# A layer's first stage from a channel-major copy of the input: squares summed by products, the scale applied by GpSimd

## The chip, the cores and the metric

The kernel runs on one core of a Trainium2 chip. A core has TensorE (PE) for matrix products, VectorE (DVE), ScalarE (ACT) and GpSimd (POOL) for work on tiles of 128 partitions, and SyncE (SP), whose queue issues nearly all transfers between HBM and the core's SBUF. Products land in PSUM. The engines run on their own, each through its instructions in order, and wait for one another by semaphores. The metric is the device time of one execution in microseconds (us); the median of the runs counts.

## What is computed

One layer of a decoder over 1024 positions of 1024 channels. What the change touches is its beginning:

```python
mod = c_act @ w_ada[l] + b_ada[l]              # c_act = silu(c)
sh1, sc1, g1, sh2, sc2, g2 = split(mod, 6)
h = rms_norm(x, pre_mix_g[l]) * (1.0 + sc1) + sh1
y = token_mixer(h, w_in[l], ...)               # begins with h @ w_in
x = x + g1 * rms_norm(y, post_mix_g[l])
...                                            # gated MLP with its own norm, shift and gain
```

`rms_norm` divides each position by the root of the mean square over its channels. All of it is float32; a product is made of three products of rounded parts (`hi` by `hi`, `hi` by `lo`, `lo` by `hi`).

## The kernel before

A product on TensorE sums over partitions, so `h` is wanted with channels on partitions: `xT`, 8 chunks of 128 channels (index `k`) by 1024 positions. `hT[t]` holds `h` for half `t` of the positions (512) in two parts: `hThi`, rounded by ACT, and the rest `hTlo`, which DVE makes by a subtraction.

The front (in the code between `front = tc.manual_schedule()` and `front.__exit__`) runs in the order in which it is written, on every engine. Behind it a planner sets the order. The front does this:

- SP's queue loads x in 8 blocks of 128 positions (`x_load`), the column constants `cv`, the rows of `w_ada` (512 KB for each of the 48 groups of modulation values, `ada_pair(k)` loads the two for chunk `k`), and the first units of `w_in`.
- For each block `b`, `x_square` (ACT, with a sum along each row) and `rstd_of` (two small POOL operations) make 1/rms; `x_turn` scales the block on DVE and transposes it in 8 pieces on PE; `x_evac` copies the pieces from PSUM to `xT`, on ACT or DVE.
- The shift and the gain of chunk `k` are `mod[:, k]` and `g_mix[:, k]`. For chunk 0 they come from products on PE (`ada_product`, 16 products of one column for each of the two); for the others from `ada_sums`: DVE multiplies the 128x1024 tile of `w_ada` by the conditioning `cb`, spread to all partitions, with a sum along each row (`ada_sum`, L168), and `shift_gain` follows in two small DVE operations.
- `h_part(k, t)` makes `h` of chunk `k`: scale and shift (DVE for chunk 0, ACT for the others), the cast to `hThi` on ACT, the rest on DVE.
- `h_chunk(k)` prepares chunk `k + 1` and sums for chunk `k + 2`, while PE runs the 48 products of chunk `k`: 8 blocks by two units of `w_in` (`kv` and `v`) by the three terms. Each product has a weight load of its own and 256 columns. `first_split` makes the two parts of the first two units, in halves: the first before chunk 0, the second in `h_chunk(0)`.

After the 384 products, `token_group` continues with the products `tg`. POOL has nothing from the last 1/rms until the front's end, but for eight tiny memsets.

Of the kernel before, what the change touches and what calls it, by code (L numbers as in the profile page):

```python
# [10 lines left out]
F32 = mybir.dt.float32  # L11
# [7 lines left out]
P = 128  # L19
# [38 lines left out]
def layer_kernel(  # L58
    ctx: ExitStack,
    tc: tile.TileContext,  # L60
    x: bass.AP,
    w_ada: bass.AP,
    c: bass.AP,
    ccol: bass.AP,
    w_vg: bass.AP,
    w_in: bass.AP,
    w_out: bass.AP,
# [11 lines left out]
    def f(ap):  # L79
        return ap.bitcast(F32)  # L80
# [12 lines left out]
    def rstd_of(dst, ssq, n):  # L93
        G.tensor_scalar(dst, ssq, 1.0 / n, EPS, op0=ALU.mult, op1=ALU.add)  # L94
        G.tensor_tensor(dst, dst, neghalf[:, : dst.shape[1]], op=ALU.pow)
# [32 lines left out]
    def block_tile(b, name):  # L128
        return mixp.tile([P, MIXC], F32, tag=f"mix{b}", name=name)
# [77 lines left out]
    xs = [block_tile(b, f"x{b}")[:, :D] for b in range(NB)]  # L207

    def x_load(b):
        nc.sync.dma_start(xs[b], x[b * P : (b + 1) * P, :])  # L210

    def ada_tile(i, j):
        i = i if i < 10 else (i - 10) ^ 1
        if i < 2:
# [25 lines left out]
    nc.scalar.dma_start(cc8, ccol)  # L240
# [16 lines left out]
    ada_pair(3)

    def x_square(b):
        A.activation(hT[1][1][:, 6:8, :], xs[b].rearrange("p (a b) -> p a b", a=2), AF.Square, accum_out=ssq[:, b : b + 1])  # L260
        rstd_of(rst[:, b : b + 1], ssq[:, b : b + 1], D)

    xps = {}

    def x_turn(b):
        V.tensor_scalar(xs[b], xs[b], rst[:, b : b + 1], None, op0=ALU.mult)
        for h in range(2):
            ps = xps[b, h] = (mm, pB)[h](f"xtp{b}")
            for i in range(4):
                T.transpose(ps[:, i * P : (i + 1) * P], xs[b][:, (4 * h + i) * P : (4 * h + i + 1) * P], ident)  # L270

    def x_evac(b, h, copy):
        copy(xT[:, 4 * h : 4 * h + 4, b * P : (b + 1) * P], xps[b, h].rearrange("p (a b) -> p a b", a=4))

    def shift_gain(k):
        c = slice(k, k + 1)
        V.tensor_tensor(mod[:, c], mod[:, c], cv[:, C_BADA + k : C_BADA + k + 1], op=ALU.add)
        V.scalar_tensor_tensor(g_mix[:, c], mod[:, 8 + k : 9 + k], cv[:, C_PREMIX + k : C_PREMIX + k + 1], gb[:, c], op0=ALU.mult, op1=ALU.add)

    def h_part(k, t):  # L280

        c = slice(k, k + 1)
        hk = xT[:, k, 512 * t : 512 * (t + 1)]
        hi, lo = (part[:, k, :] for part in hT[t])
        return (
            lambda: A.activation(hk, hk, AF.Identity, bias=mod[:, c], scale=g_mix[:, c]),
            lambda: V.tensor_scalar(hk, hk, g_mix[:, c], mod[:, c], op0=ALU.mult, op1=ALU.add),
            lambda: A.copy(hi, hk),
            lambda: V.tensor_tensor(lo, hk, f(hi), op=ALU.subtract),
        )  # L290

    C_, D_ = A.copy, V.tensor_copy
    x_square(0)
# [3 lines left out]
    A.activation(tc8, cc8, AF.Tanh, scale=0.5)  # L297
    V.scalar_tensor_tensor(cc8, tc8, 1.0, cc8, op0=ALU.add, op1=ALU.mult)
    V.tensor_scalar(cc8, cc8, 0.5, None, op0=ALU.mult)
# [6 lines left out]
    x_turn(0)  # L306
    x_square(1)
    x_turn(1)
    x_square(2)
    for h in range(2):  # L310
        A.copy(cb[:, 512 * h : 512 * (h + 1)], cbs[h])
    x_evac(0, 1, D_)
    mps = []

    def ada_product(j):

        if not mps:
            mps.append(pA("mod0"))
        for k in range(KD):
            T.matmul(mps[0][:, j : j + 1], adas[j][:, k * P : (k + 1) * P], cc8[:, k : k + 1], start=k == 0, stop=k == KD - 1)  # L320

    for b in range(2, NB):
        x_turn(b)
        if b + 1 < NB:
            x_square(b + 1)
        x_evac(b - 2, 0, C_)
        x_evac(b - 1, 1, D_ if b < 6 else C_)
        if b == 5:

            V.scalar_tensor_tensor(gb, cv[:, C_BADA + 8 : C_BADA + 16], 1.0, cv[:, C_PREMIX : C_PREMIX + 8], op0=ALU.add, op1=ALU.mult)  # L330
            ada_product(8)
        if b == 6:
            ada_product(0)
    V.tensor_tensor(mod[:, 0:1], mps[0][:, 0:1], cv[:, C_BADA : C_BADA + 1], op=ALU.add)
# [23 lines left out]
    for _ in ada_sums(1):  # L358
        pass

    def h_chunk(k):

        if k and k + 3 < KD:
            ada_pair(k + 3)
        sums = ada_sums(k + 2) if k + 2 < KD else iter(())
        if k + 1 < KD:
            for t in range(2):
                act, _, cast, rest = h_part(k + 1, t)
                act()
                cast()  # L370
                next(sums, None)
                rest()
        next(sums, None)
# [43 lines left out]

    for k in range(KD):
        h_chunk(k)
        for n, b in passes(k):  # L420
                hi, lo = hT[b // 4]
                ts = slice((b % 4) * P, (b % 4 + 1) * P)
                uh, ul = (part[:, (k % 4) * 256 : (k % 4 + 1) * 256] for part in units[2 * (k // 4) + n])
                ps = (pkv, pv)[n][b // 2][:, 256 * (b % 2) : 256 * (b % 2 + 1)]

                mm3(ps, hi[:, k, ts], lo[:, k, ts], uh, ul, k == 0 and b % 2 == 0, k == KD - 1 and b % 2 == 1)
# [885 lines left out]
def _columns(v):  # L1312
    return v.reshape(-1, P).T


def _layout(inputs):
# [30 lines left out]
        ],  # L1347
        axis=1,
    )
    w_ada = np.ascontiguousarray(g["w_ada"][0].T)  # L1350
    for j in (0, 8):

        b = slice(j * P, (j + 1) * P)
        w_ada[b] = g["w_ada"][0][:, b].reshape(KD, P, P).transpose(1, 0, 2).reshape(P, D)
    rows = np.concatenate([g["ml_i_b"][0], g["ml_f_b"][0], g["attn_sinks"][0]])[None, :]
    return {
        "x": g["x"].reshape(S, D),
        "w_ada": w_ada,
        "c": g["c"].reshape(1, D),
        "ccol": _columns(g["c"]),  # L1360
        "w_vg": w_vg,
        "w_in": np.concatenate(parts, axis=0),
        "w_out": g["w_out"][0],
# [23 lines left out]
```

## Time and profile before

| | |
|---|---|
| runs | 1128.68, 1127.90, 1127.55 us; median 1127.9 |
| profiled execution | 1128.73 us; from first to last instruction (span) 1126.7 |
| PE busy | 1110.8 us, 99% of the span |
| DVE / ACT / POOL busy | 75% / 50% / 13% |
| granted clock of TensorE, mean | 0.996 |
| first product of the front (`kv`) | 26.42 us after the span's start |
| first product behind the front (`tg`) | 75.35 us |

A row of the trace in order of time reads: start in us, duration, engine, line of the kernel, operation, what it writes and reads, shapes; in brackets the idle time of that engine before it and what ended it. A row of the chain has start, duration and the engine with tile and line. A window row has, for one stretch, the busy time and number of instructions of PE, PE's weight loads, DVE, ACT and POOL, then the granted clock as a share of full speed, the share of the DMA engines in use, and GB/s.

### The profile page before, as it was taken

To read this page: it belongs to the slowest core of one execution; us is meant where nothing else is said; L and a number is where in the kernel's file an instruction comes from. 1 tells how busy PE (TensorE), PEld (TensorE's weight loads), DVE (VectorE), ACT (ScalarE), POOL (GpSimd) and SP (SyncE) were. 2 spreads that over 40 slices of the span, in tenths; PEclk is the share of its full clock that TensorE was granted. 3 is DMA by queue.
4 is the path that set the end of the run, shared out by engine and by line. 5 is a ranking of instruction groups with operands and counts; after the bars stand their busy time and mean duration, and the time that the engine had idled before them with its cause. 6 is when DMAs were issued, how large, how long until landed. Compare 5 with 4: busy or idle time off the path is not lost.

```text
span 1126.7 us, 16175 instructions
## 1 busy us (share of the span) xinstructions
PE 1110.8 (99%) x5949; PEld 943.7 (84%) x5949; DVE 846.0 (75%) x1510; ACT 563.2 (50%) x1133; POOL 150.3 (13%) x227
## 2 busy tenths in 40 slices
PE   7999999999999999999999999999999999999997
PEld 6999998888899888877788888888888888888886
DVE  4946879857665456798897888879787877777686
ACT  6642534655535345575553545445454555454552
POOL 2012334554334100000000000000000000000021
PEclk8999999999999999999999999999999999999999
DMA  9625526242103222323333233233313359633445
GB/s 355 236 96 178 166 77 188 94 150 75 38 20 108 100 93 94 113 79 127 103 122 111 67 122 107 72 102 122 121 56 113 132 182 359 230 116 103 150 127 210
DMA packets 55166, 146.85 MB, mean 130 GB/s; under 512 B 5464, under 2 KB 5808, under 8 KB 55088
## 3 DMA queue, kind: packets, MB, share of 16 engines
q1 hardware_dynamic: 53056, 140.31, 37.2%
q10 hardware_dynamic: 2032, 5.51, 1.2%
q8 instruction: 47, 0.77, 0.3%
q14 instruction: 31, 0.25, 0.1%
HBM read 117.19 MB, written 28.61 MB: 129 GB/s over the span
## 4 chain that ended last, share of the span: by engine, by line
PE 90%; DVE 5%; ACT 2%; DMA 2%; issue 1%; POOL 0%; DVEq 0%; POOLq 0%; ACTq 0%
PE X L1036 7%; PE X L1035 7%; PE X L1037 7%; PE Y L1036 4%; PE Y L1037 4%; PE Y L1035 4%; PE dx L1217 3%; PE dx L1215 3%; PE dx L1216 3%; PE tg L89 3%; PE tg L90 3%; PE tg L91 3%; PE dz L1217 3%; PE dz L1216 3%; PE dz L1215 3%; PE y L89 3%
## 5 line engine op out<-in xcount | busy, mean ns | idle before, releaser
L94 POOL TENSOR_SCALAR rsb<-ssb 128x1 f32<-128x1 f32 x4 | 2.3, 576 | 606.8 <-ACT junk L1270 606.6
L1035 PE MATMUL X<-S,wl 128*128 128x512 f32 x156 | 62.5, 400 | 0.0
L1037 PE MATMUL X<-S,wl 128*128 128x512 f32 x156 | 61.7, 396 | 0.0
L1036 PE MATMUL X<-S,wl 128*128 128x512 f32 x156 | 61.6, 395 | 0.0
L1045 DVE SCALAR_TENSOR_TENSOR yg<-ug,cv,yg 128x1023 f32<-128x1023 f32 (+1 forms) x44 | 56.4, 1282 | 6.6 <-ACT yg L1042 6.6
L168 DVE SCALAR_TENSOR_TENSOR ada<-ada,cb 128x1024 f32<-128x1024 f32 x46 | 57.0, 1248 | 3.0 <-DMA ada<-in_w_ada_dram 3.0
L86 ACT CAST wl<-T 128x512 fp32r<-128x512 f32 x41 | 25.5, 622 | 66.1 <-PE X L1036 62.2
L1045 DVE SCALAR_TENSOR_TENSOR yv<-uv,cv,yv 128x1023 f32<-128x1023 f32 (+1 forms) x44 | 56.3, 1279 | 1.2 <-ACT yv L1042 1.2
L86 ACT CAST A<-ra 128x512 fp32r<-128x512 f32 x46 | 28.6, 621 | 49.4 <-PE dx L1217 20.1
L86 ACT CAST w<-T 128x512 fp32r<-128x512 f32 x47 | 29.1, 622 | 40.8 <-PE Z L1037 34.8
L1089 DVE TENSOR_TENSOR uv<-q,X 128x512 f32<-128x512 f32 x22 | 15.1, 687 | 41.3 <-PE X L1037 41.3
L86 DVE TENSOR_TENSOR w<-T,w 128x512 fp32r<-128x512 f32 x47 | 32.2, 689 | 15.4 <-ACT w L86 15.4
L86 DVE TENSOR_TENSOR A<-ra,A 128x512 fp32r<-128x512 f32 x46 | 31.8, 690 | 15.3 <-ACT A L86 15.3
L1217 PE MATMUL dx<-B,A 128*128 128x512 f32 x108 | 42.4, 393 | 0.0
L1216 PE MATMUL dx<-B,A 128*128 128x512 f32 x108 | 42.3, 391 | 0.0
L1215 PE MATMUL dx<-B,A 128*128 128x512 f32 x108 | 39.8, 394 | 0.0
L1037 PE MATMUL Y<-S,wl 128*128 128x512 f32 x92 | 36.4, 395 | 0.0
L1035 PE MATMUL Y<-S,wl 128*128 128x512 f32 x92 | 36.4, 395 | 0.0
L1036 PE MATMUL Y<-S,wl 128*128 128x512 f32 x92 | 36.4, 395 | 0.0
L86 ACT CAST wl<-fu 128x512 fp32r<-128x512 f32 x21 | 13.1, 622 | 46.3 <-PE Y L1036 43.4
L1036 PEld LDWEIGHTS X<-S,wl 128*128 128x128 f32 x156 | 29.3, 188 | 7.4 <-issue 0.5
L1035 PEld LDWEIGHTS X<-S,wl 128*128 128x128 f32 x156 | 29.3, 188 | 7.4 <-issue 0.5
(587 smaller groups left out, 3910.9 us busy)
## 6 DMA issues: line engine op xcount, KB each, us to landing
ada<-in_w_ada_dram SPq DMA_DIRECT2D x48, 512.0 KB, 4.2
ra<-a_dram SPq DMA_DIRECT2D x30, 512.0 KB, 3.9
fu<-in_w_up_dram SPq DMA_DIRECT2D x26, 512.0 KB, 3.5
a_dram<-yg SPq DMA_DIRECT2D x22, 512.0 KB, 3.7
rb<-in_w_down_dram SPq DMA_DIRECT2D x44, 256.0 KB, 4.4
fu_False<-in_w_up_dram SPq DMA_DIRECT2D x18, 512.0 KB, 3.5
a_dram<-s SPq DMA_DIRECT2D x11, 512.0 KB, 5.6
x<-in_x_dram SPq DMA_DIRECT2D x8, 512.0 KB, 7.5
```

What stands on the lines that cost most here:

```text
L86: return A.copy(hi, src), eng.tensor_tensor(lo, src, f(hi), op=ALU.subtract)
L89: T.matmul(ps, lh, rh, start=first, stop=False)
L90: T.matmul(ps, lh, rl, start=False, stop=False)
L91: return T.matmul(ps, ll, rh, start=False, stop=last)
L168: return V.scalar_tensor_tensor(w, w, 0.5, cb, op0=ALU.mult, op1=ALU.mult, accum_out=mod[:, j : j + 1])
L1035: T.matmul(ps, w[:, 0, ks], a[:, 0, k, :], start=st, stop=False, skip_group_check=True)
L1036: T.matmul(ps, w[:, 0, ks], a[:, 1, k, :], start=False, stop=False, skip_group_check=True)
L1037: ends = T.matmul(ps, w[:, 1, ks], a[:, 0, k, :], start=False, stop=en, skip_group_check=True)
L1045: V.scalar_tensor_tensor(t[:, sh:], src[:, : S - sh], w(tap), t[:, sh:], op0=ALU.mult, op1=ALU.add)
L1215: T.matmul(ps[tb], a[:, 0, ts], w[:, 0], start=first and r == 0, stop=False, skip_group_check=True)
L1216: T.matmul(ps[tb], a[:, 0, ts], w[:, 1], start=False, stop=False, skip_group_check=True)
L1217: ends = T.matmul(ps[tb], a[:, 1, ts], w[:, 0], start=False, stop=last and r == NP - 1, skip_group_check=True)
```

## The change

The host hands over x a second time, laid out by channels (`xt`). The front then goes as follows.

- `x_load(k)` loads chunk `k` straight into `xT`. No transposes, no evacuations.
- ACT squares the 8 chunks; DVE adds them up in `acc`. Products of `acc` with a column of ones sum over the partitions (`ss`), which gives the mean square with positions on partitions; ACT adds the epsilon, POOL takes the power (two operations of 128x4).
- 8 products of 1/rms with the identity bring it to all partitions, in PSUM (`rb`), with positions along the row. 20 products of `ones` with itself (`warm`) stand between the products for `cb` and those for `ss`.
- Chunk 0: shift and gain by `ada_sums(0)` on DVE. DVE's `h_scale` multiplies `xT` by the gain and by `rb` (read from PSUM); ACT adds the shift into `hThi`; DVE makes the rest. The rests of the first weight halves, `w0lo` and `w1lo`, move from DVE to POOL.
- Chunks 1 to 7: ACT copies `rb` to `rbc` in SBUF; POOL multiplies `xT` by it in place (`x_scale`, two halves for chunk 1, whole chunks of 128x1024 for the others). ACT then scales and shifts, casts, and DVE makes the rest, as before.
- The products of a chunk are issued in fours: `hi` by `hi` of four blocks, then `hi` by `lo`, then `lo` by `hi`.
- The loads of x come one behind the other, ahead of `cv` and the first `w_ada` tile; the tiles of `w_ada` take other buffers.

```diff
+    def x_load(k):
+        nc.sync.dma_start(xT[:, k, :], xt[k * P : (k + 1) * P, :])
...
-    def first_split(u, i):
+    def first_split(u, i, eng=V):
         raw, hi, lo = (t[:, 512 * i : 512 * (i + 1)] for t in first[u])
-        return lambda: A.copy(hi, raw), lambda: V.tensor_tensor(lo, raw, f(hi), op=ALU.subtract)
+        return lambda: A.copy(hi, raw), lambda: eng.tensor_tensor(lo, raw, f(hi), op=ALU.subtract)
...
     x_load(0)
     nc.sync.dma_start(ident, consts[:, K_ID : K_ID + P])
-    for b in range(1, 6):
-        x_load(b)
+    for k in range(1, KD):
+        x_load(k)
+    ada_pair(0, (0,))
     nc.sync.dma_start(cv, cols)
-    ada_pair(0, (0,))
-    x_load(6)
-    x_load(7)
+    first_load(0, 0)
     ada_pair(0, (1,))
-    first_load(0, 0)
+    ada_pair(1, (0,))
     first_load(1, 0)
-    ada_pair(1)
+    ada_pair(1, (1,))
...
+    def h_scale(k, ts, r):
+        V.scalar_tensor_tensor(xT[:, k, ts], xT[:, k, ts], g_mix[:, k : k + 1], r, op0=ALU.mult, op1=ALU.mult)
...
+            lambda: A.activation(hi, hk, AF.Identity, bias=sh),
+            lambda: V.scalar_tensor_tensor(lo, hk, sh, f(hi), op0=ALU.add, op1=ALU.subtract),
...
+    def x_square(k, ts):
+        A.activation((acc if k == 0 else sqs[k % 3])[:, ts], xT[:, k, ts], AF.Square)
+
+    def x_add(k, ts):
+        V.tensor_tensor(acc[:, ts], acc[:, ts], sqs[k % 3][:, ts], op=ALU.add)
...
+    for i in range(20):
+        T.matmul(warm[:, :P], ones, ones, start=True, stop=True)
...
+    for t in range(2):
+        x_add(k, halves_[t])
+        pss = pA(f"ss{t}")
+        bs = slice(4 * t, 4 * t + 4)
+        for b in range(4 * t, 4 * t + 4):
+            T.matmul(pss[:, b : b + 1], acc[:, b * P : (b + 1) * P], ones[:, 0:1], start=True, stop=True)
+        A.activation(rst[:, bs], pss[:, bs], AF.Identity, bias=eps, scale=1.0 / D)
+        G.tensor_tensor(rst[:, bs], rst[:, bs], neghalf[:, bs], op=ALU.pow)
...
+    rbs = [p("rb") for p in (mm, pB)]
+    for b in range(NB):
+        T.matmul(rbs[b // 4][:, b % 4 * P : (b % 4 + 1) * P], rst[:, b : b + 1].to_broadcast([P, P]), ident, start=True, stop=True)
...
+    for t in range(2):
+        A.copy(rbc[:, halves_[t]], rbs[t])
+
+    def x_scale(k, ts):
+        G.tensor_tensor(xT[:, k, ts], xT[:, k, ts], rbc[:, ts], op=ALU.mult)
...
+        if k + 2 < KD:
+            x_scale(k + 2, whole)
...
+        for i in range(0, len(todo), 4):
+            for term in range(3):
+                for n, b in todo[i : i + 4]:
...
+                    T.matmul(ps, h_, w_, ...)
```

What stands in a row on POOL, before: from the last 1/rms to the first work behind the front (`mix` are tiles of the attention stage, `vat` and `later` its constants).

```order
L95 TENSOR_TENSOR rst<-rst,neghalf 128x1
L587 MEMSET mix_836 128x4
...
L447 MEMSET vat 128x16
L484 MEMSET later 128x128
L485 AFFINE_SELECT later<-later 128x128
L464 TENSOR_TENSOR kr_884<-ra_2_885,rb_2_886 128x2x32
```

And in the changed kernel, from the first power on:

```order
L317 TENSOR_TENSOR rst<-rst,neghalf 128x4
L600 MEMSET mix_756 128x4
L317 TENSOR_TENSOR rst<-rst,neghalf 128x4
L238 TENSOR_TENSOR w0lo<-w0raw,w0hi 128x512
L238 TENSOR_TENSOR w1lo<-w1raw,w1hi 128x512
L350 TENSOR_TENSOR xT<-xT,rbc 128x512 x2
L350 TENSOR_TENSOR xT<-xT,rbc 128x1024 x6
L600 MEMSET mix_757 128x4
```

Ten elementwise operations, of 512 and 1024 columns, now stand there back to back; the remaining memsets come behind them.

DVE before, from the shift and gain of chunk 0 to the rests of chunk 1 (`ada` are tiles of `w_ada`, `_106` and `_107` the parts of the first half of the positions, `_108` and `_109` of the second):

```order
L287 TENSOR_SCALAR xT<-xT,gains,mod 128x512
L289 TENSOR_TENSOR hTlo_109<-xT,hThi_108 128x512
L168 SCALAR_TENSOR_TENSOR ada_145,mod<-ada_145,cb 128x1024
L168 SCALAR_TENSOR_TENSOR ada_147,mod<-ada_147,cb 128x1024
L277 TENSOR_TENSOR mod<-mod,cv 128x1
L278 SCALAR_TENSOR_TENSOR gains<-mod,cv,gb 128x1
L168 SCALAR_TENSOR_TENSOR ada_151,mod<-ada_151,cb 128x1024
L289 TENSOR_TENSOR hTlo_107<-xT,hThi_106 128x512
L168 SCALAR_TENSOR_TENSOR ada_153,mod<-ada_153,cb 128x1024
L289 TENSOR_TENSOR hTlo_109<-xT,hThi_108 128x512
```

And the same place in the changed kernel:

```order
L265 SCALAR_TENSOR_TENSOR xT<-xT,gains,rb 128x512 x2
L274 SCALAR_TENSOR_TENSOR hTlo_107<-xT,mod,hThi_106 128x512
L169 SCALAR_TENSOR_TENSOR ada_136,mod<-ada_136,cb 128x1024
L274 SCALAR_TENSOR_TENSOR hTlo_109<-xT,mod,hThi_108 128x512
L169 SCALAR_TENSOR_TENSOR ada_142,mod<-ada_142,cb 128x1024
L259 TENSOR_TENSOR mod<-mod,cv 128x1
L260 SCALAR_TENSOR_TENSOR gains<-mod,cv,gb 128x1
L169 SCALAR_TENSOR_TENSOR ada_146,mod<-ada_146,cb 128x1024
L367 TENSOR_TENSOR hTlo_107<-xT,hThi_106 128x512
L169 SCALAR_TENSOR_TENSOR ada_148,mod<-ada_148,cb 128x1024
L367 TENSOR_TENSOR hTlo_109<-xT,hThi_108 128x512
```

DVE's order from here on is the old one: sum, rest, sum, rest for each chunk. The first rests of the two weight units are gone from it, and the sums of chunk 1 now stand around the second rest of chunk 0.

More of the change, by code (lines that the diff above doesn't have):

```diff
@@ L61, in layer_kernel @@
     x: bass.AP,
+    xt: bass.AP,
     w_ada: bass.AP,
     c: bass.AP,
-    ccol: bass.AP,
     w_vg: bass.AP,
@@ L206, in layer_kernel, with ada_tile @@
     gb = cp.tile([P, KD], F32, name="gb")
[L207 to L214, printed above, removed]
+    sqs = [block_tile(i, f"sq{i}")[:, :D] for i in (0, 1, 3)]
+    acc = block_tile(2, "acc")[:, :D]
+    def x_load(k):
+        nc.sync.dma_start(xT[:, k, :], xt[k * P : (k + 1) * P, :])
+    def ada_tile(k, i, j):
+        if k % 4 == 0:
             return ap0.tile([P, D], F32, tag=f"w{i}", name=f"ada{j}")
-        return block_tile(i - 2, f"ada{j}")[:, :D]
+        return block_tile((4, 6, 0)[k % 4 - 1] + i, f"ada{j}")[:, :D]
     adas = {}
@@ L256, in layer_kernel @@
     nc.sync.dma_start(rw, rows.to_broadcast([P, 16]))
[L257 to L273, printed above, removed]
     def shift_gain(k):
@@ L278, in shift_gain @@
         V.scalar_tensor_tensor(g_mix[:, c], mod[:, 8 + k : 9 + k], cv[:, C_PREMIX + k : C_PREMIX + k + 1], gb[:, c], op0=ALU.mult, op1=ALU.add)
+    halves_ = [slice(512 * t, 512 * (t + 1)) for t in range(2)]
+    def h_scale(k, ts, r):
+        V.scalar_tensor_tensor(xT[:, k, ts], xT[:, k, ts], g_mix[:, k : k + 1], r, op0=ALU.mult, op1=ALU.mult)
     def h_part(k, t):
-        c = slice(k, k + 1)
-        hk = xT[:, k, 512 * t : 512 * (t + 1)]
+        hk = xT[:, k, halves_[t]]
         hi, lo = (part[:, k, :] for part in hT[t])
+        sh = mod[:, k : k + 1]
         return (
[L286 to L289, printed above, removed]
-        )
-    C_, D_ = A.copy, V.tensor_copy
-    x_square(0)
+            lambda: A.activation(hi, hk, AF.Identity, bias=sh),
+            lambda: V.scalar_tensor_tensor(lo, hk, sh, f(hi), op0=ALU.add, op1=ALU.subtract),
+        )
+    def x_square(k, ts):
+        A.activation((acc if k == 0 else sqs[k % 3])[:, ts], xT[:, k, ts], AF.Square)
+    def x_add(k, ts):
+        V.tensor_tensor(acc[:, ts], acc[:, ts], sqs[k % 3][:, ts], op=ALU.add)
+    whole = slice(0, S)
+    warm = pC("warm")
+    x_square(0, whole)
     A.activation(th8, ch8, AF.Tanh, scale=0.5)
     V.scalar_tensor_tensor(ch8, th8, 1.0, ch8, op0=ALU.add, op1=ALU.mult)
-    A.activation(tc8, cc8, AF.Tanh, scale=0.5)
-    V.scalar_tensor_tensor(cc8, tc8, 1.0, cc8, op0=ALU.add, op1=ALU.mult)
-    V.tensor_scalar(cc8, cc8, 0.5, None, op0=ALU.mult)
     cbs = []
@@ L322, in layer_kernel @@
[L322 to L334, printed above, removed]
@@ new lines, in layer_kernel @@
+    x_square(1, whole)
+    x_add(1, whole)
+    for k in range(2, KD - 1):
+        x_square(k, whole)
+        x_add(k, whole)
+        if k in (3, 4):
+            h = k - 3
+            A.copy(cb[:, 512 * h : 512 * (h + 1)], cbs[h])
+    k = KD - 1
+    for t in range(2):
+        x_square(k, halves_[t])
+    for t in range(2):
[6 more added lines that the diff above has]
+        G.tensor_tensor(rst[:, bs], rst[:, bs], neghalf[:, bs], op=ALU.pow)
@@ L356, in ada_sums, with h_late, cast @@
         shift_gain(k)
-    for _ in ada_sums(1):
+    for _ in ada_sums(0):
         pass
+    w0, w1 = first_split(0, 0, G), first_split(1, 0, G)
+    w0[0]()
+    w0[1]()
+    h0, h1 = h_part(0, 0), h_part(0, 1)
+    h_scale(0, halves_[0], rbs[0])
+    h0[0]()
+    h_scale(0, halves_[1], rbs[1])
+    w1[0]()
+    w1[1]()
+    h1[0]()
+    h0[1]()
+    for t in range(2):
+        A.copy(rbc[:, halves_[t]], rbs[t])
+    def x_scale(k, ts):
+        G.tensor_tensor(xT[:, k, ts], xT[:, k, ts], rbc[:, ts], op=ALU.mult)
+    for ts in halves_:
+        x_scale(1, ts)
+    second_sums = ada_sums(1)
+    next(second_sums)
+    h1[1]()
+    for _ in second_sums:
+        pass
+    def h_late(k, t):
+        hk = xT[:, k, halves_[t]]
+        hi, lo = (part[:, k, :] for part in hT[t])
+        def cast():
+            A.activation(hk, hk, AF.Identity, bias=mod[:, k : k + 1], scale=g_mix[:, k : k + 1])
+            A.copy(hi, hk)
+        return cast, lambda: V.tensor_tensor(lo, hk, f(hi), op=ALU.subtract)
     def h_chunk(k):
@@ L365, in h_chunk @@
         sums = ada_sums(k + 2) if k + 2 < KD else iter(())
+        if k + 2 < KD:
+            x_scale(k + 2, whole)
         if k + 1 < KD:
-            for t in range(2):
-                act, _, cast, rest = h_part(k + 1, t)
-                act()
+            parts = [h_late(k + 1, t) for t in range(2)]
+            for cast, rest in parts:
                 cast()
@@ L372, in h_chunk @@
                 rest()
-        next(sums, None)
+        for _ in sums:
+            pass
         if k == 0:
@@ L419, in layer_kernel @@
         h_chunk(k)
[L420 to L426, printed above, removed]
+        todo = passes(k)
+        for i in range(0, len(todo), 4):
+            for term in range(3):
+                for n, b in todo[i : i + 4]:
+                    h_ = hT[b // 4][term == 2][:, k, (b % 4) * P : (b % 4 + 1) * P]
+                    w_ = units[2 * (k // 4) + n][term == 1][:, (k % 4) * 256 : (k % 4 + 1) * 256]
+                    ps = (pkv, pv)[n][b // 2][:, 256 * (b % 2) : 256 * (b % 2 + 1)]
+                    T.matmul(ps, h_, w_, start=k == 0 and term == 0 and b % 2 == 0, stop=k == KD - 1 and term == 2 and b % 2 == 1)
     V.tensor_scalar(nsink, rw[:, 8:16], -1.0, None, op0=ALU.mult)
@@ L1357, in _layout @@
         "x": g["x"].reshape(S, D),
-        "w_ada": w_ada,
+        "xt": g["x"].reshape(S, D).T,
+        "w_ada": g["w_ada"][0].T,
         "c": g["c"].reshape(1, D),
-        "ccol": _columns(g["c"]),
         "w_vg": w_vg,
```

42 lines of the change are left out of this document (6 added, 36 removed).

## The prediction

> **What bounds the kernel now.** I read the page first: busy shares, slices, the chain of waits.
>
> ```profile
> PE 1110.8 (99%) x5949; PEld 943.7 (84%) x5949; DVE 846.0 (75%) x1510; ACT 563.2 (50%) x1133; POOL 150.3 (13%) x227
> PE   7999999999999999999999999999999999999997
> POOL 2012334554334100000000000000000000000021
> PE 90%; DVE 5%; ACT 2%; DMA 2%; issue 1%; POOL 0%; DVEq 0%; POOLq 0%; ACTq 0%
> ```
>
> TensorE is the bound everywhere but in the first slice. The order of instructions behind the front is the same in both kernels on every engine, so what the change is worth is how much earlier or later the front's last product ends and the first `tg` product starts. Next the windows of the front, the chain within it, and PE's rows in order of time.
>
> ```profile
> 10.00:20.00 10.00, 9.20 (x58) 8.41 (x57) 7.49 (x12) 9.74 (x21) 6.46 (x13) 1.00 1.03 412
> 22.00:24.00 2.00, 2.00 (x13) 2.00 (x12) 0.00 (x0) 1.10 (x2) 0.00 (x0) 0.57 1.03 414
> 26.00:28.00 2.00, 2.00 (x9) 1.52 (x8) 1.86 (x4) 1.37 (x3) 0.00 (x0) 0.50 1.03 404
> 28.00:30.00 2.00, 2.00 (x14) 2.00 (x14) 1.26 (x3) 1.10 (x2) 0.00 (x0) 0.72 0.98 395
> 40.00:50.00 10.00, 10.00 (x86) 10.00 (x85) 9.61 (x20) 6.55 (x10) 0.32 (x3) 1.00 0.60 231
> ...
> 26.42 0.58 PE L89 MATMUL kv<-w0hi,hThi 128*128 128x256 f32 x1
> 28.16 0.41 PE L89 MATMUL kv<-w0hi,hThi 128*128 128x256 f32 x1
> 28.38 0.41 PE L90 MATMUL kv<-w0lo,hThi 128*128 128x256 f32 x1
> 40.00 0.28 PE L90 MATMUL v<-w1lo,hThi 128*128 128x256 f32 x1
> 40.12 0.28 PE L91 MATMUL v<-w1hi,hTlo 128*128 128x256 f32 x1
> ...
> 36.16 0.62 DVE hTlo L289
> 36.82 0.38 PE kv L91
> 75.35 0.12 PE tg L89
> ```
>
> The window columns are PE, PEld, DVE, ACT, POOL busy, granted clock, DMA share, GB/s. DMA runs full to 20 us. The first of the 384 products (8 chunks of 48) starts at 26.42. The clock is at half from about 22.3 (0.57 in that window) to about 29.1 (0.72), where products follow each other by 0.22; at full clock by 0.12. The last stall ends at 36.82 with DVE's rest of chunk 1; from there PE is solid until `tg` starts at 75.35. In 40 to 50 DVE is busy 9.61 of 10 us and POOL 0.32. So the front can gain at its start, and it has hardly any DVE time to give away.
>
> **The change part by part.**
>
> *Earlier start.* x's last block no longer stands behind `cv` and one `ada` block (152 and 512 KB), and the transposes go.
>
> ```profile
> ada<-in_w_ada_dram SPq DMA_DIRECT2D x18, 512.0 KB, 7.5
> cv<-in_cols_dram SPq DMA_DIRECT2D x1, 152.0 KB, 8.9
> 16.16 1.06 ACT L260 ACTIVATE hTlo<-x 128x1024 fp32r<-128x1024 f32 x1 [0.18 <-DMA x<-in_x_dram]
> 17.02 1.06 PE L270 MATMUL xtp<-ident,x 128*128 128x128 f32 x8 [0.61 <-DVE x L266]
> 24.61 1.95 PE L270 MATMUL xtp<-ident,x 128*128 128x128 f32 x8
> 19.18 1.84 PE L320 MATMUL mod<-cc,ada 128*128 128x1 f32 x16
> 25.74 0.62 ACT L288 CAST hThi<-xT 128x512 fp32r<-128x512 f32 x1 [2.65 <-DVE xT L287]
> 26.39 0.69 DVE L289 TENSOR_TENSOR hTlo<-xT,hThi 128x512 fp32r<-128x512 f32 x1
> 362.40 1.23 DVE L86 TENSOR_TENSOR wolo<-woraw,wohi 128x1024 fp32r<-128x1024 f32 x1 [1.59 <-ACT wohi L86]
> 5.86 0.19 ACT L297 ACTIVATE tc<-cc 128x8 f32<-128x8 f32 x1
> 32.83 0.82 ACT L286 ACTIVATE xT<-xT,mod,gains 128x512 f32<-128x512 f32 x1 [2.89 <-DVE gains L278]
> 30.18 2.30 DVE ada L168 x4
> 32.66 0.14 DVE gains L278
> L95 POOL TENSOR_TENSOR sums<-sums,neghalf 128x4 f32<-128x4 f32 x8 | 10.2, 1276 | 0.7
> ```
>
> The seventh x block was there at 16.1; without the 664 KB ahead of it (at 412 GB/s 1.65 us) the eighth, 1.27 us behind it, is there at about 15.7. Then in a chain: two half squares (0.62 each), DVE's last two adds of 512 columns (0.69, overlapping), which it reaches at 17 since its adds of 1024 take 1.2 each: all squares summed at 18.1. Two times 4 one-column products, 8 instructions each (half of 1.84): 18.8 and 19.7. ACT's small step 0.2 and POOL's power for 4 columns (1.0 to 1.28; the second comes behind an `ada` sum): 20.4 and 21.6. 1/rms to all partitions, 8 instructions a half (1.06 at full, 1.95 at half clock): 23.0 for the second. DVE's `h_scale` and ACT's `hThi` (0.69; 0.62 to 0.82) follow the first half, at 21.5: first product at about 23.0, at 24.7 if the clock is at half: 1.7 to 3.4 us earlier. The 20 extra products on `ones` fill PE while it waits. The `ada` sums of chunk 0 (two in 2.30) replace 32 small products; they run on DVE while the powers are taken, and only `h_scale` waits for them. What else goes or comes (the accumulator reads of the squares, `ccol`, one small load less on ACT's queue; `ada` loads of chunk 3 issued behind the adds on SP, which reaches them at 20 anyway) has no one waiting for it.
>
> *Order of the products.* By term in fours instead of three per block: every product had a weight load of its own and keeps it, so I take 0; no row shows the other order, ends 4% of 46 us either way, 1.9.
>
> *GpSimd scales.* POOL now holds `w0lo`, `w1lo`, two halves of `x_scale(1)` and six whole blocks, one behind the other without a wait (its order shows that), where it was idle:
>
> ```profile
> POOL mix L587 <- DVE ada L168: 40.1, 8, 19.2
> 363.95 2.40 POOL L86 TENSOR_TENSOR wolo<-woraw,wohi 128x1024 fp32r<-128x1024 f32 x1 [3.93 <-ACT wohi L86]
> 365.46 1.97 DVE L86 TENSOR_TENSOR wolo<-woraw,wohi 128x1024 fp32r<-128x1024 f32 x1 [0.79 <-ACT wohi L86]
> 326.28 1.26 POOL L751 TENSOR_TENSOR qw<-U,yq 128x512 f32<-128x512 f32 x1
> 326.36 1.21 DVE L786 TENSOR_TENSOR mtmp<-mtmp,gcol 128x4 f32<-128x4 f32 x1
> ...
> 161.94 1.50 POOL L546 TENSOR_SCALAR_AFFINE_SELECT pT<-pT 128x512 f32<-128x512 f32 x1
> 162.88 1.64 DVE L168 SCALAR_TENSOR_TENSOR ada<-ada,cb 128x1024 f32<-128x1024 f32 x1
> ...
> 194.65 2.50 POOL L94 TENSOR_SCALAR rsta<-ssq 128x1 f32<-128x1 f32 x1 [1.97 <-ACT asq L562]
> 195.88 1.21 DVE L168 SCALAR_TENSOR_TENSOR ada<-ada,cb 128x1024 f32<-128x1024 f32 x1
> ```
>
> These rows carry the forecast. A DVE operation on four columns takes 1.21 us and ends with the POOL instruction that began before it. DVE's 1.23 us subtraction (362.40) takes 1.97 when POOL is in its 2.40 us one: 0.89 of waiting until POOL ends at 366.35, then its own time. An operation on one engine that reads two operands from SBUF waits for the whole instruction on the other; and they take turns: POOL at 161.94 waits for one `ada` sum, gets in ahead of the next, and that one takes 1.64.
> [...]
>
> DVE's operations here (`ada` sums, the rests `hTlo`, the small `mod` and `gains`) all read two from SBUF. From 23.6, when `w1lo` starts behind ACT's cast, to the last rest of chunk 1, POOL holds the ports 3 x 1.3 + 6 x 2.40 = 18.3 us, and DVE has to do 4 `ada` sums (1.15), 4 rests (0.6) and two small ones (0.14): 7.3. In turns that is 25.6 us, so that rest is ready at about 49.2 instead of 36.8. `gains` of chunk 1, behind six POOL and six DVE turns (1.3, 0.6, 1.3, 1.15, 1.3, 0.6, 2.4, 1.15, 2.4, 0.14, 2.4, 0.14), comes at 38.5, so ACT's `hThi` (0.82 and 0.62) at 40. PE, done with chunk 0 at 32, does 20 of chunk 1's products between 40 and 49 and waits. Queued behind the blocked rests on DVE are the second halves of `w0lo` and `w1lo`; SP's `w3raw` and `w4raw` wait for those, needed only 15 us later. After 49.2 POOL is through and DVE needs 3.8 per chunk (2 sums, 2 rests, 2 small) against PE's 48 x 0.12 = 5.8.
> Left for PE then: 28 + 6 x 48 = 316 products at 0.12: 37.9, to 87.1. The clock: after such gaps it should stand at half, as it did from 22.3 to 29.1 in rows where PE was even partly busy. At half for 3.4 to 6.8 us (half of that stretch, and all of it) each us costs 0.44 (0.12 for 0.215): 1.5 to 3.0; I take 1.7, since 20 products have run shortly before. `tg` starts at 88.8.
> [...]
>
> Sum: 88.8 - 75.35 = 13.4 us later, all of it in PE idle time between about 32 and 49. The profiled execution took 1128.73 (span 1126.7), so 1142.1; it is 0.8 above the median of the runs, 1127.9, so the median to expect is 1141.3. Bounds of this case: if the small operations pass in one turn, or POOL's are 0.1 shorter, 1.0 to 2.4 less; if POOL takes 2.6 and the clock returns late, 2.8 more: 1138 to 1145.
>
> **The rivals.**
> *VectorE keeps the ports.* For it: POOL's 128x1 operation at 194.65 took 2.50 us, through two `ada` sums in a row. Then POOL gets in only where DVE waits for ACT or a load; `x_scale(1)` starts at 30 and chunk 1's last rest comes at 36 to 38, but `x_scale(2)`, `(4)` and `(6)` then wait until DVE has nothing to do: PE waits some 3 us at chunk 2, 1 at chunks 4 and 6, 3 at chunk 7. With the first product at 24.7, 46.1 of products and 2.7 of half clock `tg` starts at 81.5 to 82.9: 6.2 to 7.5 slower, 1134 to 1135.5. Against it: 161.94 and 326.36.
> *No lock for these operations* (the other side). POOL's multiplications run beside DVE's; they then end ahead of need (6 x 2.40 against 5.8 per chunk), and only the start counts: 23.0 + 384 x 0.12 = 69.1, plus 0 to 2.6 for the clock: 3.7 to 6.3 faster, 1121.5 to 1124.2. For it: POOL stands at 13% of the span, and PE waits for DVE in today's front (36.16). Against: every row above. It decides if a DVE `ada` sum takes 1.2 while `x_scale` runs.
> *A hold of part of an instruction.* If POOL keeps the ports for a quarter to two fifths of its time, the loss eats just the earlier start, within 0.2% (2.3 us, about what a measurement of this kernel tells from no change). Against: 365.46, where DVE waited to the end.
>
> **How the numbers follow.** Turns: 0.68. VectorE keeps the ports: 0.17. Partial hold: 0.06 (two thirds of it within 0.2%). No lock: 0.09. Slower 0.68 + 0.17 + 0.02 = 0.87, same 0.04, faster 0.09. The likeliest is 1141.3, its own range 1138 to 1145; the range given, 1132 to 1145, takes in the second case too and leaves out the last two and a part of the tails.
>
> **What would show it.** First product at 23 to 25. POOL's x-scale operations listed at 2.4 to 4 us each, one behind another, from 25 to 48; DVE's `ada` sums there at 2.5 to 3.6 instead of 1.22, a 128x1 `gains` at over 2. PE idle for some 6 us at 33 and again until about 49, the clock at half shortly behind; `tg` at 87 to 91. Wrong if DVE's sums stay at 1.2 in 25 to 48, or if PE's idle time there is under 5 us.

## The result, and the profile after

| | before | changed |
|---|---|---|
| median | 1127.75 us (1127.55 to 1128.68) | 1139.12 us (1136.38 to 1140.76) |
| ratio | | 1.0097, interval 1.0075 to 1.0118 |
| profiled execution (span) | 1128.73 (1126.7) | 1139.87 (1138.1) |

The change costs 11.4 us, 1.0%. The forecast was slower, 1141.3, with 1138 to 1145 for its case and 1132 to 1145 with the second case. From the changed kernel's page, the lines of busy shares and of the slices that answer to those of before, and the group of the `ada` sums, which was L168 and 57.0 us for 46 there:

```profile
PE 1109.9 (98%) x5925; PEld 943.3 (83%) x5925; DVE 862.0 (76%) x1505; ACT 559.2 (49%) x1119; POOL 169.1 (15%) x223
PE   7599999999999999999999999999999999999997
POOL 3602233634533200000000000000000000000011
L169 DVE SCALAR_TENSOR_TENSOR ada<-ada,cb 128x1024 f32<-128x1024 f32 x48 | 65.0, 1363 | 1.8 <-DMA ada<-in_w_ada_dram 1.6
```

PE's busy time is 0.9 us shorter and the span is 11.4 us longer: the time is idle time of PE, and it lies in the second slice (5 tenths), where POOL is now at 6. Two more sums don't explain 8 us in their group: some take longer. Now VectorE's rows there in order of time, and POOL's:

```profile
21.62 0.75 DVE L265 SCALAR_TENSOR_TENSOR xT<-xT,gains,rb 128x512 f32<-128x512 f32 x1 [1.79 <-PE rb L323]
23.79 1.75 DVE L274 SCALAR_TENSOR_TENSOR hTlo<-xT,mod,hThi 128x512 fp32r<-128x512 f32 x1
25.46 2.30 DVE L169 SCALAR_TENSOR_TENSOR ada<-ada,cb 128x1024 f32<-128x1024 f32 x1
27.70 1.76 DVE L274 SCALAR_TENSOR_TENSOR hTlo<-xT,mod,hThi 128x512 fp32r<-128x512 f32 x1
29.38 3.40 DVE L169 SCALAR_TENSOR_TENSOR ada<-ada,cb 128x1024 f32<-128x1024 f32 x1
32.83 2.17 DVE L259 TENSOR_TENSOR mod<-mod,cv 128x1 f32<-128x1 f32 x1
34.93 2.37 DVE L260 SCALAR_TENSOR_TENSOR gains<-mod,cv,gb 128x1 f32<-128x1 f32 x1
37.23 1.21 DVE L169 SCALAR_TENSOR_TENSOR ada<-ada,cb 128x1024 f32<-128x1024 f32 x1
38.89 2.34 DVE L367 TENSOR_TENSOR hTlo<-xT,hThi 128x512 fp32r<-128x512 f32 x1 [0.45 <-ACT hThi L366]
41.15 3.40 DVE L169 SCALAR_TENSOR_TENSOR ada<-ada,cb 128x1024 f32<-128x1024 f32 x1
44.49 2.81 DVE L367 TENSOR_TENSOR hTlo<-xT,hThi 128x512 fp32r<-128x512 f32 x1
...
18.27 2.10 POOL L317 TENSOR_TENSOR rst<-rst,neghalf 128x4 f32<-128x4 f32 x1 [17.78 <-ACT rst L316]
21.38 1.26 POOL L238 TENSOR_TENSOR w0lo<-w0raw,w0hi 128x512 fp32r<-128x512 f32 x1
25.18 21.58 POOL L350 TENSOR_TENSOR xT<-xT,rbc 128x512 f32<-128x512 f32 x8 [0.19 <-ACT rbc L346]
```

A sum's own time is 1.21 (the one at 37.23); beside POOL's whole chunks it takes 3.40. An operation on a single column (0.14 to 0.21 alone) takes 2.17 and 2.37. So a whole chunk holds VectorE for about 2.2 us (3.40 - 1.21). POOL's eight multiplications run from 25.18 to 46.76 without a gap. `h_scale` at 21.62 reads its second operand from PSUM and isn't held (0.75), though POOL's `w0lo` stands beside it from 21.38 to 22.64.

What TensorE makes of it, in its rows, then `tg` from the chain, two windows of the clock, and the waits:

```profile
23.18 1.23 PE L439 MATMUL kv<-w0hi,hThi 128*128 128x256 f32 x4
38.91 1.22 PE L439 MATMUL kv<-w0hi,hThi 128*128 128x256 f32 x4 [7.24 <-ACT hThi L366]
47.36 1.23 PE L439 MATMUL kv<-w0hi,hTlo 128*128 128x256 f32 x4 [3.87 <-DVE hTlo L367]
...
87.47 0.12 PE tg L89
...
50.00:52.00 2.00, 2.00 (x11) 2.00 (x10) 2.00 (x4) 1.39 (x2) 0.00 (x0) 0.50 1.03 399
52.00:54.00 2.00, 2.00 (x16) 2.00 (x16) 2.00 (x5) 1.47 (x3) 0.00 (x0) 0.82 0.96 355
...
ACT xT L365 <- DVE gains L260: 24.2, 6, 11.8
PE kv L439 <- ACT hThi L366: 7.2, 1, 7.2
PE kv L439 <- DVE hTlo L367: 4.2, 2, 3.9
```

The first product comes 3.2 us earlier than before. PE is then idle for 7.24 us until 38.91 (behind `gains`, for which ACT waited 11.8 us) and for 3.87 until 47.36 (behind the last rest of chunk 1), and behind that second wait the clock is at half until about 53 (four products take 1.05 us at 51.80 and 0.64 at 53.15). `tg` starts at 87.47, 12.1 us later.

### The profile page after: what moved, and what is told of

Its sections match the earlier page's. It is cut to its first block, busy times and chain, and to the rows that moved or that the text cites. A ratio compares the mean times of both kernels' runs of the same rounds, so it can differ in the third digit from the quotient of the medians.

```text
span 1138.1 us, 16104 instructions
## 1 busy us (share of the span) xinstructions
PE 1109.9 (98%) x5925; PEld 943.3 (83%) x5925; DVE 862.0 (76%) x1505; ACT 559.2 (49%) x1119; POOL 169.1 (15%) x223
## 4 chain that ended last, share of the span: by engine, by line
PE 92%; DVE 3%; DMA 1%; ACT 1%; issue 1%; POOL 0%; SPq 0%; DVEq 0%; POOLq 0%; ACTq 0%
PE X L1049 7%; PE X L1048 7%; PE X L1050 7%; PE Y L1049 4%; PE Y L1050 4%; PE Y L1048 4%; PE dx L1230 3%; PE dx L1228 3%; PE dx L1229 3%; PE tg L89 3%; PE tg L90 3%; PE tg L91 3%; PE dz L1230 3%; PE dz L1228 3%; PE dz L1229 3%; PE y L89 3%
## 5 line engine op out<-in xcount | busy, mean ns | idle before, releaser
L169 DVE SCALAR_TENSOR_TENSOR ada<-ada,cb 128x1024 f32<-128x1024 f32 x48 | 65.0, 1363 | 1.8 <-DMA ada<-in_w_ada_dram 1.6
L86 DVE TENSOR_TENSOR A<-ra,A 128x512 fp32r<-128x512 f32 x46 | 31.7, 688 | 15.7 <-ACT A L86 15.7
```

Source lines behind the costliest of these rows:

```text
L86: return A.copy(hi, src), eng.tensor_tensor(lo, src, f(hi), op=ALU.subtract)
L169: return V.scalar_tensor_tensor(w, w, 0.5, cb, op0=ALU.mult, op1=ALU.mult, accum_out=mod[:, j : j + 1])
```

## The experiments

The theory: each of GpSimd's multiplications holds up VectorE's operations on two SBUF operands, for about its whole length (2.2 us by the rows above); these get their turn between them, and PE waits for VectorE. (The expectations speak of a shared port; no run shows one, the runs show durations.) The rivals: the front's other edits cost the time; GpSimd's results are simply late; VectorE has too much to do; any work of GpSimd does it.

**Taking the multiplications out** (the chunks then are not divided by the rms).

```diff
     def x_scale(k, ts):
-        G.tensor_tensor(xT[:, k, ts], xT[:, k, ts], rbc[:, ts], op=ALU.mult)
+        pass
```

> The changed kernel with GpSimd's multiplications of xT by rbc left out (chunks 1 to 7 stay undivided by the rms; everything else is there). Theory (GpSimd and VectorE take turns at a shared port): VectorE's sums in 25 to 48 us are back at about 1.2 us, the last rest of chunk 1 is there at about 32 instead of 47.3, and tg starts at 70.8 to 72.3: 1123 to 1125. Rival (the other edits of the front cost the time: the order of products, the powers, the clock at half): PE still stands for several us and the time stays above 1135.

1122.92 us, ratio to before 0.9966 (0.9953 to 0.9979), with `tg` from 69.5 us, both a little better than expected. VectorE's sums and single columns are back at their own time:

```profile
26.37 1.21 DVE L169 SCALAR_TENSOR_TENSOR ada<-ada,cb 128x1024 f32<-128x1024 f32 x1
27.70 0.21 DVE L260 SCALAR_TENSOR_TENSOR gains<-mod,cv,gb 128x1 f32<-128x1 f32 x1
31.20 0.69 DVE L367 TENSOR_TENSOR hTlo<-xT,hThi 128x512 fp32r<-128x512 f32 x1
29.47 0.74 PE L439 MATMUL kv<-w0hi,hThi 128*128 128x256 f32 x4 [0.67 <-ACT hThi L366]
```

The rest of the change is worth some 4 us (0.9966), and the multiplications cost about 15 on top of it (1.0097 less 0.9966). Chunk 1's last rest is there at 31.9, as expected. The rival of the other edits falls.

**The same kind of work, with nobody waiting for it, in the kernel before.**

```diff
     x_evac(7, 1, C_)
+    for _ in range(7):
+        G.tensor_tensor(ubk[:, 4:], xT[:, 7, :], cb, op=ALU.mult)
```

> The kernel before, with seven multiplications of 128x1024 added on GpSimd behind the last copy into xT (two operands read from SBUF, the result used by nobody). Theory: they hold the port 7 x 2.4 = 16.8 us, taken in turns with VectorE's operations; VectorE's last rest of chunk 1 moves from 36.8 to about 50 and tg to 87 to 90: 1139 to 1143. Rival (the multiplications of the changed kernel cost by their data, since ScalarE waits for them): nobody waits for these, so 1127.5 to 1128.5.

1140.63 us, 1.0112 (1.0095 to 1.0129). VectorE's rows, and two of PE's:

```profile
28.72 3.42 DVE L168 SCALAR_TENSOR_TENSOR ada<-ada,cb 128x1024 f32<-128x1024 f32 x1
32.07 3.36 DVE L168 SCALAR_TENSOR_TENSOR ada<-ada,cb 128x1024 f32<-128x1024 f32 x1
35.47 2.17 DVE L277 TENSOR_TENSOR mod<-mod,cv 128x1 f32<-128x1 f32 x1
39.33 0.58 PE L89 MATMUL kv<-w0hi,hThi 128*128 128x256 f32 x1 [6.55 <-ACT hThi L288]
59.83 0.39 PE L91 MATMUL kv<-w0hi,hTlo 128*128 128x256 f32 x1 [2.26 <-DVE hTlo L289]
```

Seven operations whose results nobody reads cost 12.7 us: no lateness of data is needed. The place was not quite as expected: the last three stood behind memsets that wait for `ada` sums, so chunk 1's last rest came at 43.4 and not at 50, and a part of the loss came later, as at 59.83.

**GpSimd work that reads nothing, and that reads one operand,** at the same place.

```diff
+    G.tensor_tensor(ubk[:, 4:8], xT[:, 7, :4], cb[:, :4], op=ALU.mult)
+    for _ in range(16):
+        G.memset(ubk[:, 4:], 0.0)
```

> The kernel before, with sixteen memsets of 128x1024 added on GpSimd at the same place (they write SBUF and read nothing). [...] Rival (any work of GpSimd takes the port): sums of 2 us and more, and 1134 to 1142, by how long a memset takes.

```diff
+    for _ in range(7):
+        G.tensor_scalar(ubk[:, 4:], xT[:, 7, :], 2.0, None, op0=ALU.mult)
```

> The kernel before, with seven operations of 128x1024 on GpSimd at the place of the seven multiplications (1140.6), but with one operand from SBUF and a constant. If it is reading SBUF that takes the port, VectorE's sums beside them take longer than 1.3 us by the rest of such an operation, and with about 1.2 to 1.4 us for each the time rises by a third to a half as much: 1131 to 1136. If only operations with two operands from SBUF meet at it, the sums stay at 1.2 us: 1127 to 1129.

The memsets: 1128.05 us, 1.0006 (0.9996 to 1.0016), not the 1134 to 1142 of the rival. One operand: 1130.64, 1.0021 (1.0008 to 1.0034), just below the range expected. First POOL's row of the memsets and a sum beside them, then POOL's first row, two sums and a single column of the other kernel:

```profile
19.08 16.86 POOL L353 MEMSET ubk<- 128x1024 f32 x16
29.31 1.22 DVE L168 SCALAR_TENSOR_TENSOR ada<-ada,cb 128x1024 f32<-128x1024 f32 x1
...
28.26 9.18 POOL L352 TENSOR_SCALAR ubk<-xT 128x1024 f32<-128x1024 f32 x3 [9.02 <-ACT xT L273]
28.33 2.06 DVE L168 SCALAR_TENSOR_TENSOR ada<-ada,cb 128x1024 f32<-128x1024 f32 x1
30.32 1.21 DVE L168 SCALAR_TENSOR_TENSOR ada<-ada,cb 128x1024 f32<-128x1024 f32 x1
31.58 0.87 DVE L277 TENSOR_TENSOR mod<-mod,cv 128x1 f32<-128x1 f32 x1
```

Sixteen memsets, 17 us of GpSimd, cost nothing; an operation with one operand from SBUF holds VectorE for 0.85 us (2.06 - 1.21). So it takes more than a busy GpSimd that writes to SBUF: a sum took 1.22 beside the memsets, against 2.06 beside an operation that reads one operand from SBUF and 3.42 beside one that reads two. How long the hold lasts differs: a multiplication of two operands holds VectorE for 2.2 us, about its whole length (2.40 in the prediction's row). But three operations of one operand fill 9.18 us, some 3 us each, and the second sum, at 30.32, runs beside them in its own time. Why they hold for less than their rows are long stays open.

**The same multiplications, one for each chunk** in place of six back to back (`behind` makes the first wait until the second is done).

```diff
     def x_scale(k, ts):
-        G.tensor_tensor(xT[:, k, ts], xT[:, k, ts], rbc[:, ts], op=ALU.mult)
+        return G.tensor_tensor(xT[:, k, ts], xT[:, k, ts], rbc[:, ts], op=ALU.mult)
...
-        if k + 2 < KD:
-            x_scale(k + 2, whole)
...
-            for cast, rest in parts:
+            for t, (cast, rest) in enumerate(parts):
                 cast()
                 next(sums, None)
-                rest()
+                done = rest()
+                if t == 0 and k + 2 < KD:
+                    behind(x_scale(k + 2, whole), done)
```

> The changed kernel with the same GpSimd multiplications, but from chunk 2 on each held back until the first rest of the chunk before has been made, so one for each chunk's turn and not six back to back. Theory: the chain to the last rest of chunk 1 loses five turns of 2.4 us and ends at 35 to 36.5; from then a chunk takes 2.4 + 3.8 = 6.2 us at the port against PE's 5.8, so tg starts at 75.5 to 78: 1128 to 1131. Rival (it is the sum of GpSimd's time that counts, wherever it stands): 1137 to 1140 as in the changed kernel. Rival (GpSimd's results come late for ScalarE, the port is no matter): later still, above 1139.

1134.76 us, 1.0065 (1.0053 to 1.0078): 3.6 us better than the changed kernel by the ratios, with the same GpSimd work, but worse than the theory's 1128 to 1131 and better than its two rivals' ranges. Each multiplication now meets one sum and one rest:

```profile
34.49 2.84 DVE L367 TENSOR_TENSOR hTlo<-xT,hThi 128x512 fp32r<-128x512 f32 x1
41.55 2.87 DVE L367 TENSOR_TENSOR hTlo<-xT,hThi 128x512 fp32r<-128x512 f32 x1
48.58 2.86 DVE L367 TENSOR_TENSOR hTlo<-xT,hThi 128x512 fp32r<-128x512 f32 x1
```

These chunks come every 7.0 us, against the 6.2 expected: the reckoning had left out the rests of the weight units on VectorE (1.2 to 1.4 us in these chunks). With PE at 5.8 a chunk it waits again and again, and `tg` starts at 81.8. Placement matters. VectorE is busy or held for 21.47 of the 22 us from 34 to 56, so the time of both engines together per chunk sets the pace there.

**VectorE does the scaling itself.**

```diff
     def x_scale(k, ts):
-        G.tensor_tensor(xT[:, k, ts], xT[:, k, ts], rbc[:, ts], op=ALU.mult)
+        pass
...
-            parts = [h_late(k + 1, t) for t in range(2)]
+            h_scale(k + 1, whole, rbc)
+            parts = [h_part(k + 1, t) for t in range(2)]
```

> The changed kernel with the scaling of chunks 1 to 7 moved from GpSimd to VectorE: one operation of 1024 columns a chunk that multiplies by gain and 1/rms together; ScalarE then needs one step less. GpSimd keeps w0lo and w1lo. Theory: VectorE has 3.8 + 1.15 = 4.95 us a chunk against PE's 5.8, without turns to wait for; last rest of chunk 1 at about 33.5, tg at 71 to 72.5: 1123.5 to 1125.5, faster than both kernels. Rival (VectorE simply has too much to do in this front): the chunks come every 6 us or more and the time is 1130 or above.

1125.57 us, 0.9985 (0.9976 to 0.9995): faster than both kernels, at the upper end of what was expected. (The edit also takes one step for each half chunk off ScalarE.) With `w0lo` and `w1lo` on VectorE too:

```diff
-    w0, w1 = first_split(0, 0, G), first_split(1, 0, G)
+    w0, w1 = first_split(0, 0), first_split(1, 0)
```

> As the one before, and the rests w0lo and w1lo back on VectorE too, so that GpSimd does only the two powers. Theory: VectorE gets 1.4 us more work before chunk 1, but loses the 1.2 us that its rest of chunk 0 waited for w1lo; within 1 us of the one before: 1123.5 to 1126. If turns at the port cost more than their length, this is the faster of the two by 1 us or more.

1126.22 us, 0.9992 (0.9983 to 1.0): the same within the intervals, just above the range expected. One multiplication of 1024 columns by gain and 1/rms takes VectorE 1.3 us, where it lost 2.2 to GpSimd's; the rival of too much work on VectorE falls as the cause. It is what remains, though: PE's longest wait in the front is now 1.30 us.

```profile
27.74 1.29 DVE L265 SCALAR_TENSOR_TENSOR xT<-xT,gains,rbc 128x1024 f32<-128x1024 f32 x1
29.84 0.74 PE L432 MATMUL kv<-w0hi,hThi 128*128 128x256 f32 x4 [1.30 <-ACT hThi L273]
```

**Another order for VectorE there:** scale a chunk right behind its gain, and both rests ahead of the sums.

```diff
+    h_scale(1, whole, rbc)
...
-            h_scale(k + 1, whole, rbc)
             parts = [h_part(k + 1, t) for t in range(2)]
             for cast, rest in parts:
                 cast()
+            if k == 0:
                 next(sums, None)
+            for cast, rest in parts:
                 rest()
         for _ in sums:
             pass
+        if k + 2 < KD:
+            h_scale(k + 2, whole, rbc)
```

> As the kernel in which VectorE scales chunks 1 to 7 (1125.6), with another order on VectorE: chunk k + 2 is scaled right behind its gain, and the two rests of chunk k + 1 come ahead of the sums for chunk k + 2. VectorE's work is the same. That kernel still has PE idle for 1.3 us at chunk 1 and some 0.1 to 0.3 us once or twice a chunk up to 57 us, waiting for hThi and hTlo. Theory (what is left there is the place of the rests in VectorE's queue): these go, tg starts 1 to 2 us earlier, 1123.5 to 1125. Rival (VectorE's time a chunk, 5 to 6.2 us against PE's 5.8, is the bound): the waits only move, 1125 to 1126.5.

1129.02 us, 1.001 (1.0001 to 1.0018): a miss, 2.8 us worse by the ratios. The 1.30 stays, and a wait that I hadn't thought of comes in:

```profile
55.21 0.74 PE L430 MATMUL v<-w3lo,hThi 128*128 128x256 f32 x4 [2.93 <-DVE w3lo L86]
```

VectorE reaches the rest of weight unit `w3` only behind two sums and a scale; PE wants it first. Behind that wait the clock is at half from about 56.2 to 59.6 (four products take 1.06 us at 56.28 and 0.64 at 59.67). The old order was the better one for this.

**The order of the products,** in the kernel before (in fours, as changed; this is the edit shown) and in the kernel just shown (three by three, as before).

```diff
-        for n, b in passes(k):
...
-                mm3(ps, hi[:, k, ts], lo[:, k, ts], uh, ul, ...)
+        for i in range(0, len(todo), 4):
+            for term in range(3):
+                for n, b in todo[i : i + 4]:
...
+                    T.matmul(ps, h_, w_, ...)
```

> The kernel before, with the front's products issued in fours by term, as the changed kernel has them, and nothing else changed. The prediction put this edit at 0, with ends 1.9 us to both sides: 1127.9, between 1126 and 1129.8.

> The same kernel with the front's products in the old order, three terms for each block. The edit alone, made in the kernel before, gave 0.9989 (0.9979 to 0.9998); if that is the order's doing, this kernel is 1 to 1.5 us slower than the one with the products in fours; if the prediction's 0 is right, it is within 0.7 us of it.

In fours before: 1126.48, 0.9989 (0.9979 to 0.9998). Three by three in the other: 1129.18, 1.0007 (0.9998 to 1.0017), against 1.001 (1.0001 to 1.0018) in fours. So 1.2 us (0.2 to 2.4) in the one, and nothing in the other. In the latter's rows the order only moves a wait:

```profile
30.57 0.75 PE L430 MATMUL kv<-w0hi,hThi 128*128 128x256 f32 x4 [1.30 <-ACT hThi L273]
...
29.68 0.39 PE L89 MATMUL kv<-w0hi,hThi 128*128 128x256 f32 x1 [0.71 <-ACT hThi L273]
30.73 0.39 PE L91 MATMUL kv<-w0hi,hTlo 128*128 128x256 f32 x1 [0.55 <-DVE hTlo L274]
```

In fours (first row) PE needs `hTlo` only behind eight other products and doesn't wait for it; three by three it waits 0.71 and 0.55, together as much.

**The 20 products of ones,** left out of the changed kernel, and of the one in which VectorE scales.

```diff
-    for i in range(20):
-        T.matmul(warm[:, :P], ones, ones, start=True, stop=True)
```

> The changed kernel without the 20 products of ones with itself. If they keep the clock up, ss and rb run at half clock, and the first product comes 0.5 to 1.7 us later; VectorE's chain behind it moves by as much at most: 1139 to 1141. If the clock is at full anyway while x comes in: no change, 1139.

> The kernel in which VectorE scales chunks 1 to 7 (1125.6, 0.9985 of before, 0.9976 to 0.9995), without the 20 products of ones with itself. There the clock stood at full from 14 us to 56 us. In the changed kernel leaving these products out gave 1142.2, 3 us more than the 1139.1 of the changed kernel, in runs of another call and with turns at the port beside. If they keep the clock up, or PE's earlier products wait for less, the time is 1 to 3 us higher here too: 1126.6 to 1128.6. If the 3 us came from the turns falling out differently, no change: 1125.0 to 1126.2.

1142.21 us, 1.0127 (1.0111 to 1.0142), above what was expected, where the changed kernel had 1.0097; and 1128.77, 1.0009 (1.0 to 1.0018), just above what was expected, where VectorE's scaling with them had 0.9985. They are worth some 2.7 us there (0.0024 of 1128; 1.2 to 4.2 by both intervals). The rows of PE without them, and a window of that; then the same with them:

```profile
7.77 2.12 PE L295 MATMUL cb<-ch,ident 8*128 8x128 f32 x9
16.18 3.58 PE L312 MATMUL ss<-ones,acc 128*128 128x1 f32 x16 [6.29 <-DVE acc L282]
20.01 3.53 PE L320 MATMUL rb<-ident,rst 128*128 128x128 f32 x16 [0.26 <-POOL mix L590]
16.00:20.00 4.00, 3.58 (x16) 3.49 (x16) 3.38 (x9) 0.48 (x3) 1.57 (x2) 1.00 1.02 410
...
16.82 1.95 PE L315 MATMUL ss<-ones,acc 128*128 128x1 f32 x16
19.50 2.31 PE L323 MATMUL rb<-ident,rst 128*128 128x128 f32 x16 [0.74 <-POOL mix L593]
```

Without them the sums of squares and the spreading of 1/rms take 3.58 and 3.53 us instead of 1.95 and 2.31, and the first product starts at 23.7 instead of 22.3; `tg` starts 1.7 us later. The 6.29 us of idle time ahead isn't what slows them: the products before it were as slow (9 in 2.12 us, as 16 in 3.53 in the row of `rb`). PE was at half from its first product to the last ones of `rb`, which end at 23.5; the four products at 23.68 take 0.74, about what the first four take with the extra products (0.73). With these PE came to full between 14 and 16: the window from 12 to 14 has 11 products, the next one 18. The other microsecond or so of the difference lies behind the front, in no one place that I could pin down; it stays open.

## Why the prediction was right, step by step

- *Earlier start.* First product at 23.0 to 24.7 forecast, 23.18 measured. (The 3.2 us against the first product before is one pair of profiles: in the profiles here it starts at 24.4 to 26.4 with the old front and at 22.1 to 23.8 with the new one.) Two errors in it cancel: x's last block landed at 14.3 instead of 15.7, and the first power took 2.10 us instead of 1.0 (beside an `ada` sum, the second one came on time with 1.02). That this step alone would bring 3.7 to 6.3 us, as the rival without a lock had it, is what taking the multiplications out gave: 4.5 by the medians, 3.8 by the ratio.
- *Extra products fill PE while it waits.* Costed at nothing, with no value of their own. That step was under-read: without them PE runs at half up to about 23 instead of 14 to 16, and the start is 1.4 us later in the kernel where VectorE scales (0.6 in the changed one, 23.75 against 23.18). The sum had 1.06 to 1.95 for a half of `rb`; it is 1.2 with them (2.31 for both) and 1.8 without (3.53).
- *Order of the products: 0, ends 1.9.* Near enough: 0.16 us between two kernels that differ in it alone; in the kernel before a gain of 1.2, with an interval that reaches from 0.2 to 2.4.
- *GpSimd and VectorE in turns.* Right in kind and in its signs: sums of 2.3 to 3.4, a single column at 2.17 and 2.37, all of POOL's operations through before chunk 1's last rest, 20 products between 38.91 and 43.5 as forecast. Mis-sized: the last rest at 47.3 instead of 49.2. The price of a whole chunk on POOL was taken from a row of 2.40; here it holds VectorE 2.15 to 2.2 (3.40 and 3.36 less 1.21), which for six is 1.2 to 1.5 of the 1.9. Turns aren't strict either: the sum at 37.23 got in right behind VectorE's `gains`. The forecast has POOL hold ports for 18.3 us: no run shows ports, or a lock on them; the runs show how long an operation takes beside another (a sum 3.40 us, 1.21 alone; a single column 2.17, 0.16 alone).
- *316 products and the clock.* 37.9 + 1.7 = 39.6 forecast; from 47.36 to 87.47 it is 40.1, with the clock at half until about 53: 2.2 above the 37.9 where 1.7 was put.
- *Sum.* `tg` at 88.8 forecast, 87.47 measured. Behind it the changed kernel is 0.7 us quicker than before (1138.1 - 87.47 against 1126.7 - 75.35). Both together are 2.0 of the 2.2 us between 1142.1 and the profiled 1139.87; the rest lies outside the spans.
- *VectorE keeps the ports* (the second case) didn't happen: POOL ended its last multiplication at 46.76, in turn with VectorE. *Partial hold* neither, for the multiplications: each holds VectorE for 2.15 to 2.2 us, nearly the 2.40 forecast for the whole. For operations of one operand it isn't excluded (0.85 of some 3 us).

## What to carry to other kernels

Before work is moved to GpSimd because it is idle, look at which operations stand on VectorE at that time: here those that read two operands from SBUF shared one budget with GpSimd's multiplications of SBUF operands (3.40 us for a sum of 1.21), and a small VectorE operation paid for a whole one of these (2.17 and 2.37 us for one column). An elementwise product of 1024 columns was cheaper as 1.3 us of VectorE's own time than as 2.2 us of GpSimd's beside it; of the 4.5 us that the new front is worth without any scaling (1127.42 to 1122.92), 1.85 were kept that way. Where work must go to GpSimd there, three things came cheaper here: work that reads nothing (the memsets, 1.0006), an operation of VectorE with one operand from PSUM (0.75 us beside `w0lo`, in two kernels, and 0.75 alone), and multiplications that are spaced out (3.6 us).

## What was not expected of the hardware

The granted clock can read full where PE runs at half. In the kernel without the 20 products the window from 16 to 20 reads 1.00, while 16 products take 3.58 us against 1.95, and the 9 products at 7.77, in 2.12 us, were as slow. In the changed kernel the trace's first record of the clock is the rise to full, at 15.2 us, and the view counts a stretch without a record as full: the window from 12 to 14 reads 1.00 there with 11 products, and the one from 16 to 18 reads 1.00 with 21. So early in these spans the durations tell the clock, and that number doesn't.

Beside the memsets, with which operations on two operands kept their time (sums 1.22 us, rests 0.69), operations of another kind took longer, with a single tensor operand and constants of each partition. A multiplication and addition on 512 columns takes 0.55 us before, and 1.36 here (the next one, at 27.32, 0.64); of two multiplications on 1024 columns, 0.75 each before, one took about twice that:

```profile
18.22 2.36 DVE L266 TENSOR_SCALAR x<-x,rst 128x1024 f32<-128x1024 f32 x2
23.41 1.36 DVE L287 TENSOR_SCALAR xT<-xT,gains,mod 128x512 f32<-128x512 f32 x1
```

What makes these longer is not shown, and no other run tests it.
